# A decoder step in float32 on one core: the variance and the first products of every LayerNorm's refinement kept in PSUM

## The chip, the cores and the metric

One core of one Trainium2 chip runs the whole step as one program. The metric is the device time of one execution in microseconds, as the median of several. 0.2% of it, 2.3 us, is about what a measurement of this kernel can tell from no change.

## The reference

Two layers, each a token mixer and a gated ConvFFN, and behind each of the four a LayerNorm of the residual sum. Layer 0 mixes by sliding-window attention, layer 1 by gated linear attention (GLA). 512 prompt tokens and 8 decode tokens go through, 1024 features each.

```
def layer_norm(x, g, b):
    mu = mean(x);  var = mean((x - mu)**2)
    return (x - mu) * rsqrt(var + LN_EPS) * g + b

for i in range(2):
    m = attention(x) if i == 0 else gla(x)        # with state and cache for the decode tokens
    x = layer_norm(ALPHA * x + m, ...)
    x = layer_norm(ALPHA * x + conv_ffn(x), ...)
```

## The kernel before

Tokens lie in the free dimension, features in the 128 partitions. The 520 tokens are two groups: `a` has 256 and `b` has 264. Weights come as units of 128 output features (512 KB each); TensorE multiplies a unit with one group into an `accp` tile of PSUM, of which there are four. A float32 product is three passes of split operands (`wh`, `wl` for the weights, `xh`, `xl` for the activations), 24 matmuls of 256 or 264 columns for a unit of depth 1024. A new unit comes through a `raw` buffer, from which ScalarE (ACT) rounds `wh` (L167, L181) and VectorE (DVE) takes the rest, `wl` (L170, L183).

Group `a` runs up to five units ahead of group `b`; a method `order` writes that order out. Work that depends on a product is put into a queue of generators and emitted some units later. The framework then schedules the emitted instructions by its own model of time, so that each engine has one fixed list and waits at its head. A PSUM tile is given out in that schedule when an older one of the same name is released.

PSUM has eight banks: four `accp`, and four small ones: `sc` twice, `tp` and `pv` once each. `sc` also holds the attention scores, the first mean estimate of a norm (L256), and in GLA the product of the decay (`gla_decay`, L745: `z` times `wa2`).

`ln_end` ends a norm for one group. TensorE makes the mean `e1` and the mean square `e2` (L290), ACT squares the mean (`q`), DVE forms the negated variance `nv = (q - eps) - e2` (L306), ACT takes Ln and Exp of it to a first reciprocal root `r` (L315, L316), and three DVE operations refine it by one Newton step and leave the factor `rp` in the `pv` bank (L322, L323, L325). GpSimd (POOL) subtracts the mean from six of the eight feature blocks meanwhile (L305). Then DVE scales each block (L352), ACT writes `xh` (L353), DVE writes `xl` (L354), and the next unit's product can read them. `ln_end` is called eight times: four norms by two groups. `last` is true for the two calls of the final norm, which already take a form of their own.

After the FFN norm of layer 0, GLA starts. Its first unit is a small product of rank 16 (`gla_rank`, L736), which ACT copies to `z`; `gla_decay` makes `z` into decay factors by a chain of small operations: the product L745, `dmn` (L749, L753), `de` (L750 to L752), a scan `dcum` (L754), `eb`, `ep`, `em`. `q_a` (L779) and `k_a` (L786) need `ep` and `em` and release their `accp` tiles. Group `a` runs its units rank, q, k, v0, v1 and g0 before group `b` runs its rank product. ACT's copies L803 (`v_a`) release the tiles of v0 and v1.

Of the kernel before, what the change touches and what calls it, by code (L numbers as in the profile page):

```python
# [97 lines left out]
class Net:  # L98
# [186 lines left out]
    def ln_end(self, g, i, last=False):  # L285
# [6 lines left out]
                nc.tensor.matmul(e, self.ones_a, rest, start=False, stop=True)  # L292
        t = lambda name, b=1: self.ln.tile([P, NT - 256], F32, name=name, bufs=b)[:, :n]
        mu, q, nv, r = t("mu"), t("msq"), t("nv"), t("r")
        if last:

            nv, vr = self.mtile("sc")[:, :n], self.mtile("sc")[:, :n]
        if last:
# [15 lines left out]
                    nc.vector.tensor_tensor(x[:, m], x[:, m], e1, op=ALU.subtract)  # L314
        nc.scalar.activation(r, nv, AF.Ln, scale=-1.0)  # L315
        self.exp = nc.scalar.activation(r, r, AF.Exp, scale=-0.5).ins  # L316
        if last:
            nc.vector.tensor_tensor(vr, nv, r, op=ALU.mult)
            q = nv
            nc.vector.scalar_tensor_tensor(q, vr, 0.5, r, op0=ALU.mult, op1=ALU.mult)  # L320
        else:
            nc.vector.tensor_tensor(q, r, r, op=ALU.mult)  # L322
            nc.vector.scalar_tensor_tensor(q, q, 0.5, nv, op0=ALU.mult, op1=ALU.mult)  # L323
# [848 lines left out]
```

## Time and profile before

| | |
|---|---|
| Median of three runs | 1134.33 us (1134.12 to 1135.64) |
| The profiled execution: time, span | 1135.32 us, 1133.6 us |
| TensorE (PE) busy in the span | 1103.5 us |
| VectorE (DVE) busy | 778.8 us |
| ScalarE (ACT) busy | 565.4 us |
| GpSimd (POOL) busy | 320.2 us |
| Granted TensorE clock, mean | 0.993 |

The profiled execution lies 1.7 us above its span and 1.0 us above the median. A busy TensorE is not one at its peak, since the ends of matmuls are modelled: what counts there is the distance from start to start and the gaps with a named releaser.

### The profile page before, as it was taken

The numbers are of one execution on the slowest core, as the hardware profiler recorded it, in microseconds if no ns is written. First come the engines' busy times: TensorE is split into PE (matmuls) and PEld (weight loads), VectorE is DVE, ScalarE is ACT, GpSimd is POOL, SyncE is SP. The second block draws the span as 40 slices with busy tenths as digits, with TensorE's granted clock in tenths as the row PEclk, the third lists the DMA queues.
The fourth block names the chain that finished last, engine by engine and source line by source line (L and its number), as shares of the span: only waits on it lengthen the run. The fifth ranks groups of instructions, "written<-read, shape, count | busy, mean of one in ns | idle before, by whom it ended". The sixth has DMA issues, their size and how long they took to land.

```text
span 1133.6 us, 22916 instructions
## 1 busy us (share of the span) xinstructions
PE 1103.5 (97%) x8806; PEld 1053.7 (93%) x8806; DVE 778.8 (69%) x1626; ACT 565.4 (50%) x1251; POOL 320.2 (28%) x591
## 2 busy tenths in 40 slices
PE   8998999999999999999999999999999999999996
PEld 7997799999999999999899999899999999999995
DVE  7897679755665566568867778779755665566565
ACT  5677556524553245435455556356524553245433
POOL 3575584400110010255211101274400110001253
PEclk9999999999999999999899999999999999999999
DMA  7553023333233223242124365432333223223222
GB/s 239 152 176 99 17 76 94 112 97 127 94 98 108 93 97 110 75 134 92 58 90 146 120 177 160 138 111 94 113 95 129 94 95 110 95 95 111 76 64 76
DMA packets 53804, 122.81 MB, mean 108 GB/s; under 512 B 6808, under 2 KB 27328, under 8 KB 53696
## 3 DMA queue, kind: packets, MB, share of 16 engines
q1 hardware_dynamic: 51536, 119.47, 33.0%
q10 hardware_dynamic: 2160, 1.89, 0.5%
q8 instruction: 69, 1.13, 0.4%
q14 instruction: 39, 0.32, 0.1%
HBM read 108.67 MB, written 8.47 MB: 103 GB/s over the span
## 4 chain that ended last, share of the span: by engine, by line
PE 73%; DVE 12%; DMA 7%; ACT 3%; issue 2%; POOL 2%; SPq 1%; ACTq 0%; DVEq 0%; POOLq 0%
PE accp L221 15%; PE accp L198 15%; PE accp L200 15%; PE accp L202 15%; PE accp L222 8%; DMA vb<-dv 3%; DMA raw<-in_w_qkv 1%; DVE xs_a L354 1%; DVE wl L183 1%; DMA qs<-hl 1%; DVE sgla L909 1%; DVE wl L170 1%; DMA raw<-in_w_up 1%; DVE de L924 1%; DVE x_a L352 1%
## 5 line engine op out<-in xcount | busy, mean ns | idle before, releaser
L170 DVE TENSOR_TENSOR wl<-raw,wh 128x1024 fp32r<-128x1024 f32 (+2 forms) x172 | 207.0, 1205 | 103.9 <-ACT wh L167 103.0
L167 ACT ACTIVATE wh<-raw 128x1024 fp32r<-128x1024 f32 (+2 forms) x168 | 173.7, 1034 | 202.2 <-PE accp L200 187.6
L198 PE MATMUL accp<-xh_b,wh 128*128 128x264 f32 x976 | 272.5, 279 | 1.9 <-ACT xh_b L353 1.9
L202 PE MATMUL accp<-xh_b,wl 128*128 128x264 f32 x976 | 270.8, 277 | 0.0
L200 PE MATMUL accp<-xl_b,wh 128*128 128x264 f32 x960 | 266.5, 278 | 0.0
L221 PE MATMUL accp<-xs_a,wh 128*128 128x512 f32 x576 | 196.3, 382 | 0.0
L198 PEld LDWEIGHTS accp<-xh_b,wh 128*128 128x128 f32 x976 | 184.8, 189 | 3.4 <-ACT xh_b L353 2.5
L202 PEld LDWEIGHTS accp<-xh_b,wl 128*128 128x128 f32 x976 | 184.5, 189 | 0.9 <-issue 0.6
L200 PEld LDWEIGHTS accp<-xl_b,wh 128*128 128x128 f32 x960 | 181.6, 189 | 2.5 <-issue 0.4
L222 PE MATMUL accp<-xs_a,wl 128*128 128x256 f32 x576 | 145.4, 273 | 0.0
L198 PE MATMUL accp<-hh_b,wh 128*128 128x264 f32 x480 | 133.4, 278 | 1.7 <-ACT hh_b L228 1.2
L200 PE MATMUL accp<-hl_b,wh 128*128 128x264 f32 x480 | 133.7, 279 | 0.3 <-DVE hl_b L593 0.2
L202 PE MATMUL accp<-hh_b,wl 128*128 128x264 f32 x480 | 132.9, 277 | 0.0
L221 PEld LDWEIGHTS accp<-xs_a,wh 128*128 128x128 f32 x576 | 109.1, 189 | 11.4
L222 PEld LDWEIGHTS accp<-xs_a,wl 128*128 128x128 f32 x576 | 110.2, 191 | 1.9
L198 PE MATMUL accp<-xs_a,wh 128*128 128x256 f32 x400 | 107.5, 284 | 1.5 <-ACT wh L167 0.8
L200 PE MATMUL accp<-xs_a,wh 128*128 128x256 f32 x384 | 102.8, 281 | 0.4 <-DVE xs_a L229 0.3
L198 PEld LDWEIGHTS accp<-hh_b,wh 128*128 128x128 f32 x480 | 90.9, 189 | 2.4 <-ACT hh_b L228 1.6
L200 PEld LDWEIGHTS accp<-hl_b,wh 128*128 128x128 f32 x480 | 90.8, 189 | 1.8 <-DVE hl_b L593 0.4
L202 PEld LDWEIGHTS accp<-hh_b,wl 128*128 128x128 f32 x480 | 90.7, 189 | 0.2
L232 POOL COPY hist<-aext 128x2 f32<-128x2 f32 x44 | 10.0, 227 | 282.3 <-DVE aext L640 276.2
L198 PEld LDWEIGHTS accp<-xs_a,wh 128*128 128x128 f32 x400 | 77.1, 193 | 3.0 <-ACT wh L167 1.2
(338 smaller groups left out, 2509.2 us busy)
## 6 DMA issues: line engine op xcount, KB each, us to landing
raw<-in_w_up SPq DMA_DIRECT2D x88, 512.0 KB, 3.4
raw<-in_w_down SPq DMA_DIRECT2D x32, 512.0 KB, 3.4
raw<-in_w_gla SPq DMA_DIRECT2D x24, 512.0 KB, 3.4
raw<-in_w_mix_o SPq DMA_DIRECT2D x16, 512.0 KB, 3.9
raw<-in_w_down SPq DMA_DIRECT2D x16, 384.0 KB, 3.1
qs<-hl SPq DMA_DIRECT2D x64, 64.0 KB, 2.1
sgla<-in_state_gla SPq DMA_DIRECT2D x16, 256.0 KB, 2.7
vb<-dv SPq DMA_DIRECT2D x16, 256.0 KB, 3.9
```

Of the source, the lines that this page charges most:

```text
L167: nc.scalar.activation(h[:, c], r[:, c], AF.Copy)
L170: nc.vector.tensor_tensor(l[:, c], r[:, c], h[:, c].bitcast(F32), op=ALU.subtract)
L183: self.nc.vector.tensor_tensor(l, r, h.bitcast(F32), op=ALU.subtract)
L198: nc.tensor.matmul(o, h[:, ks], xh, start=k == 0, stop=False)
L200: nc.tensor.matmul(o, h[:, ks], xl, start=False, stop=False)
L202: nc.tensor.matmul(o, l[:, ks], xh, start=False, stop=not tail and k == nt - 1)
L221: both = lambda: nc.tensor.matmul(o, h[:, ks], in_turn(rs[:, k].rearrange("p t q j -> p t (q j)")), start=k == 0, stop=last)
L222: low = lambda: nc.tensor.matmul(o[:, :P], l[:, ks], in_turn(rh[:, k]), start=False, stop=False)
L352: v = nc.vector.scalar_tensor_tensor(x[:, m], x[:, m], sc(m), rp, op0=ALU.mult, op1=ALU.mult)
L354: xl = nc.vector.scalar_tensor_tensor(g.xl[:, m], parted(x[:, m]), bi(m), g.xh[:, m].bitcast(F32), op0=ALU.add, op1=ALU.subtract)
L909: late(nc.vector.scalar_tensor_tensor(s[:, j], vb[:, j], kraw[:, b:b + 1], s[:, j], op0=ALU.mult, op1=ALU.add))
L924: nc.vector.reciprocal(e, e)
```

## The change

The flag that chose the two PSUM tiles and the other grouping of the Newton step for the final norm alone is set for all norms. For the six other calls, `nv` moves from SBUF to an `sc` bank; the first product of the refinement becomes `nv * r` into a second `sc` bank (`vr`), in place of `r * r` in SBUF; the second becomes `vr * 0.5 * r` into the bank of `nv`, in place of `(r * r) * 0.5 * nv` in SBUF. The number of instructions is the same. Nothing else is edited.

```
         mu, q, nv, r = t("mu"), t("msq"), t("nv"), t("r")
-        if last:
+        banks = True
+        if banks:
             nv, vr = self.mtile("sc")[:, :n], self.mtile("sc")[:, :n]
...
-        if last:
+        if banks:
             nc.vector.tensor_tensor(vr, nv, r, op=ALU.mult)
             q = nv
             nc.vector.scalar_tensor_tensor(q, vr, 0.5, r, op0=ALU.mult, op1=ALU.mult)
         else:
             nc.vector.tensor_tensor(q, r, r, op=ALU.mult)
             nc.vector.scalar_tensor_tensor(q, q, 0.5, nv, op0=ALU.mult, op1=ALU.mult)
```

Each of these norms now takes both `sc` banks, from its variance to its factor. The schedule is made anew with that, and instructions move at one place above all: the FFN norm of layer 0 for group `b`, beside the start of GLA for group `a`. Line numbers behind L294 are higher by one in the changed kernel.

TensorE there, before: the decay's product L745 stands just ahead of the mean products of group `b` (the L205 and L198 rows are products of group `a`'s units).

```order
L200 MATMUL accp<-xs_a,wh 128x256
L205 MATMUL accp<-xs_a,wl 128x256 x3
L745 MATMUL sc<-z_a,wa_7008 128x256
L290 MATMUL tp<-s_b,ones_a 128x264
L205 MATMUL accp<-xs_a,wl 128x256
L290 MATMUL pv<-s_b,ones_a 128x264
```

And in the changed kernel, where the same product (L746) stands 39 rows further on, as the second instruction of unit g0:

```order
L200 MATMUL accp<-xs_a,wh 128x256
L205 MATMUL accp<-xs_a,wl 128x256 x8
L198 MATMUL accp<-xs_a,wh 128x256
L746 MATMUL sc<-z_a,wa_7016 128x256
L200 MATMUL accp<-xs_a,wh 128x256
L198 MATMUL accp<-xs_a,wh 128x256
```

It needs a bank of `sc`, and waits for the DVE operation L321, the last that reads `vr`. The other units' rows around it are unchanged up to group `b`'s rank product.

VectorE at the same place, before: the norm of `b` (L306, L322, L323, L325, L352) and the decay of `a` (L749, L753, L754) take turns.

```order
L749 TENSOR_SCALAR dmn<-sc,par 128x256
L306 SCALAR_TENSOR_TENSOR nv<-msq,pv 128x264
L314 TENSOR_TENSOR x_b<-x_b,tp 128x264 x2
L183 TENSOR_TENSOR wl<-raw,wh 128x1024
L322 TENSOR_TENSOR msq<-r 128x264
L753 TENSOR_TENSOR dmn<-dmn,de 128x256
L323 SCALAR_TENSOR_TENSOR msq<-msq,nv 128x264
L754 SCALAR_TENSOR_TENSOR dcum<-reset,dmn 128x256
L325 SCALAR_TENSOR_TENSOR pv<-msq,r 128x264
L758 COPY bl<-dcum 128x2
L841 COPY ebl<-eb 128x1
L352 SCALAR_TENSOR_TENSOR x_b<-x_b,par,pv 128x264 x8
```

After: the norm goes through in one piece, and the decay follows it.

```order
L307 SCALAR_TENSOR_TENSOR sc<-msq,pv 128x264
L315 TENSOR_TENSOR x_b<-x_b,tp 128x264 x2
L183 TENSOR_TENSOR wl<-raw,wh 128x1024
L319 TENSOR_TENSOR sc<-sc,r 128x264
L321 SCALAR_TENSOR_TENSOR sc<-sc,r 128x264
L326 SCALAR_TENSOR_TENSOR pv<-sc,r 128x264
L353 SCALAR_TENSOR_TENSOR x_b<-x_b,par,pv 128x264 x8
L355 SCALAR_TENSOR_TENSOR xl_b<-x_b,par,xh_b 128x264 x3
L750 TENSOR_SCALAR dmn<-sc,par 128x256
L355 SCALAR_TENSOR_TENSOR xl_b<-x_b,par,xh_b 128x264 x5
L754 TENSOR_TENSOR dmn<-dmn,de 128x256
L755 SCALAR_TENSOR_TENSOR dcum<-reset,dmn 128x256
```

ScalarE there, before: `eb` (L756, which needs the decay's scan) stands ahead of the first `xh_b` and of the second copy `v_a`.

```order
L752 ACTIVATE de<-de,eps 128x256
L803 COPY v_a<-accp 128x256
L756 ACTIVATE eb<-dcum 128x4
L353 ACTIVATE xh_b<-x_b,par 128x264 x2
L803 COPY v_a<-accp 128x256
L353 ACTIVATE xh_b<-x_b,par 128x264 x6
L762 ACTIVATE ep<-dcum 128x256
L763 ACTIVATE em<-dcum 128x256
L738 COPY z_b<-accp 128x264
```

After: the whole chain of `de`, `eb`, `ep` has moved behind the eight `xh_b`.

```order
L317 ACTIVATE r<-r 128x264
L804 COPY v_a<-accp 128x256
L354 ACTIVATE xh_b<-x_b,par 128x264 x3
L804 COPY v_a<-accp 128x256
L354 ACTIVATE xh_b<-x_b,par 128x264 x5
L751 ACTIVATE de<-sc,par 128x256
L752 ACTIVATE de<-de 128x256
L753 ACTIVATE de<-de,eps 128x256
L739 COPY z_b<-accp 128x264
L167 ACTIVATE wh<-raw 128x1024
L757 ACTIVATE eb<-dcum 128x4
L763 ACTIVATE ep<-dcum 128x256
```

Behind this place the instructions of all of GLA, some 1800 rows of TensorE, stand in a new order, with the same work, up to the second or third unit of layer 1's FFN; from there on TensorE has the same rows again. In the norm of layer 1's mixer, which lies in that stretch, group `a`'s scalings and splits (L353, L355) are mixed more finely with the other group's residual sums. At the attention norm of layer 0 and in group `a`'s half of the FFN norm of layer 0, the order of DVE and ACT is that of before, operation for operation.

## Rows read from the trace of the kernel before

**Rows 1.** The page's first part: busy time, share and instructions by engine.
```profile
PE 1103.5 (97%) x8806; PEld 1053.7 (93%) x8806; DVE 778.8 (69%) x1626; ACT 565.4 (50%) x1251; POOL 320.2 (28%) x591
```

**Rows 2.** What TensorE waited for, whole span: total us, times, longest.
```profile
PE accp L736 <- ACT v_a L803: 2.6, 1, 2.6
...
PE accp L198 <- ACT xh_b L353: 1.9, 2, 0.9
...
PE tp L290 <- DVE s_b L282: 1.0, 3, 0.4
...
PE accp L205 <- DVE xs_a L354: 0.5, 1, 0.5
```

**Rows 3.** Stretches: PE, PEld, DVE, ACT, POOL busy (count); clock, DMA share, GB/s.
```profile
541.00:556.00 15.00, 12.33 (x55) 10.27 (x54) 12.06 (x32) 7.79 (x18) 0.51 (x1) 0.66 0.15 54
556.00:745.00 189.00, 186.77 (x1563) 177.20 (x1563) 141.54 (x333) 98.56 (x254) 35.22 (x48) 1.00 0.43 136
1111.00:1114.00 3.00, 3.00 (x29) 3.00 (x29) 2.62 (x7) 0.99 (x3) 3.00 (x5) 1.00 0.00 0
6.00:9.00 3.00, 1.94 (x11) 1.23 (x10) 2.06 (x5) 2.13 (x6) 1.13 (x3) 1.00 1.05 339
```

**Rows 4.** TensorE in order of time, 531 to 556 us: start, duration, instruction.
```profile
531.52 0.60 PE L745 MATMUL sc<-z_a,wa 128*128 128x256 f32 x2
...
540.99 1.06 PE L205 MATMUL accp<-xs_a,wl 128*128 128x256 f32 x8
544.64 3.13 PE L736 MATMUL accp<-xh_b,wh 128*128 128x264 f32 x8 [2.59 <-ACT v_a L803]
...
550.55 1.22 PE L794 MATMUL sc<-q_a,k_a 128*128 128x128 f32 x4
...
552.92 0.56 PE L198 MATMUL accp<-xs_a,wh 128*128 128x256 f32 x1
...
555.60 0.28 PE L198 MATMUL accp<-xh_b,wh 128*128 128x264 f32 x1
```

**Rows 5.** VectorE in order of time, 537 to 547 us.
```profile
537.33 1.78 DVE L183 TENSOR_TENSOR wl<-raw,wh 128x1024 fp32r<-128x1024 f32 x1
539.04 0.97 DVE L322 TENSOR_TENSOR msq<-r 128x264 f32<-128x264 f32 x1
...
540.83 0.98 DVE L323 SCALAR_TENSOR_TENSOR msq<-msq,nv 128x264 f32<-128x264 f32 x1
...
542.33 0.41 DVE L325 SCALAR_TENSOR_TENSOR pv<-msq,r 128x264 f32<-128x264 f32 x1
...
543.66 2.48 DVE L352 SCALAR_TENSOR_TENSOR x_b<-x_b,par,pv 128x264 f32<-128x264 f32 x6
```

**Rows 6.** ScalarE in order of time, 542 to 552 us.
```profile
542.44 0.21 ACT L756 ACTIVATE eb<-dcum 128x4 f32<-128x4 f32 x1 [3.86 <-DVE dcum L754]
...
544.24 0.35 ACT L803 COPY v_a<-accp 128x256 f32<-128x256 f32 x1
544.49 2.64 ACT L353 ACTIVATE xh_b<-x_b,par 128x264 fp32r<-128x264 f32 x6
...
550.79 1.06 ACT L167 ACTIVATE wh<-raw 128x1024 fp32r<-128x1024 f32 x1
```

**Rows 7.** VectorE in order of time: group `a`'s FFN norm of layer 0.
```profile
516.41 0.60 DVE L322 TENSOR_TENSOR msq<-r 128x256 f32<-128x256 f32 x1 [0.27 <-ACT r L316]
516.94 0.41 DVE L250 TENSOR_TENSOR x_b<-x_b,accp 128x264 f32<-128x264 f32 x1
...
517.92 0.85 DVE L325 SCALAR_TENSOR_TENSOR pv<-msq,r 128x256 f32<-128x256 f32 x1
```

**Rows 8.** VectorE in order of time: group `a`'s final norm, with PSUM tiles.
```profile
1111.98 0.43 DVE L318 TENSOR_TENSOR sc<-sc,r 128x256 f32<-128x256 f32 x1 [0.31 <-ACT r L316]
1112.44 0.43 DVE L320 SCALAR_TENSOR_TENSOR sc<-sc,r 128x256 f32<-128x256 f32 x1
```

**Rows 9.** The page's fifth part, costliest groups: busy, mean ns of one; idle before, releaser.
```profile
L170 DVE TENSOR_TENSOR wl<-raw,wh 128x1024 fp32r<-128x1024 f32 (+2 forms) x172 | 207.0, 1205 | 103.9 <-ACT wh L167 103.0
```

More of the change, by code (lines that the diff above doesn't have):

```diff
@@ L294, in ln_end @@
         mu, q, nv, r = t("mu"), t("msq"), t("nv"), t("r")
-        if last:
+        banks = True
+        if banks:
             nv, vr = self.mtile("sc")[:, :n], self.mtile("sc")[:, :n]
@@ L316, in ln_end @@
         self.exp = nc.scalar.activation(r, r, AF.Exp, scale=-0.5).ins
-        if last:
+        if banks:
             nc.vector.tensor_tensor(vr, nv, r, op=ALU.mult)
```

## The prediction

> **What bounds the kernel now.** The page's first part says TensorE: 1103.5 of 1133.6 us [rows 1]. A busy TensorE is not one at its peak, so I looked next for stretches of few matmuls. Between 556 and 745 us, in GLA, 1563 matmuls start in 189 us, one every 0.121 us, at clock 1.00. [...] 55 at 0.121 us need 6.7 us, so 8.3 us are lost in that one place, where group `b`'s FFN norm of layer 0 meets GLA's start. TensorE's waits give its start: 2.59 us ahead of group `b`'s rank product L736, the longest wait in the list, put down to the copy `v_a` [rows 2, 4].
>
> ScalarE shows why that copy is late. It started at 544.24, behind two `xh_b` and behind `eb`, for which the engine had waited 3.86 us [rows 6]. `eb` needs the scan of group `a`'s decay, which took turns on VectorE with the three slow Newton operations of `b`: 0.97 us at 539.04, 0.98 at 540.83, 0.41 at 542.33 [rows 5]. The rank product, which then started at 544.64, had 16 matmuls, and took until 550.55 because it was fed by `xh_b` and `xl_b` one block at a time. The clock fell meanwhile: at 552.92 a matmul of 256 columns takes 0.56 us, at 555.60 it is 0.28 again [rows 4].
>
> **The change, part by part.**
>
> *The operations themselves.* Same count, so only durations matter. The same norm formula with PSUM tiles stands in the final norm: 0.43 us each, 0.46 from start to start [rows 8], and POOL was busy for all 3.00 us around it [rows 3]. The old ones take 0.97 and 0.98 while POOL is busy; POOL works only 0.51 us after 541 [rows 3], and the third one, behind that, takes 0.41 [rows 5]. So what is saved is the slowing beside POOL, not the operation. For group `a`, before: 516.41 to 517.92+0.85 = 518.77, or 2.36 us, with one residual sum between (0.34 to the next start) [rows 7]. After: 3 x 0.45 + 0.34 = 1.69. Each such chain is shorter by 0.67 us. Bounds: nothing, if the new ones are slowed like the old; 1.0, if the residual sum slips out of the chain.
>
> The rows say that with PSUM such an operation costs 0.43 us where one undisturbed with SBUF takes 0.41, a difference of 0.02 us [rows 5, 8]. [...]
>
> *The place at GLA's start.* The order of the work moves here: the decay's product now waits for a bank of `sc` until the norm's second Newton operation, so the norm of `b` runs through and the decay follows. I walk through it with today's times, then shift. VectorE's `wl` begins at 537 and ends at 538.6 or so (1.78 us from 537.33 today, 0.4 sooner without the decay's `dmn` ahead of it). Three operations of 0.45 end at 539.95, where today the factor was ready at 542.75 [rows 5]. The first scaling (0.41 each, 2.48 for six) starts at 540.0 instead of 542.85, the first `xh_b` at 540.4 (0.44 each, 2.64 for six [rows 6]). The second `v_a` stands behind three of them: 540.4 + 1.3 + 0.35 = 542.1. Eight matmuls of 256 columns take 1.06 us, one alone 0.28: (1.06 - 0.28) / 7 = 0.112 from start to start. Unit g0 ends at 540.99 + 8 x 0.112 = 541.9 today [rows 4]; with the decay's product in it and its wait for the bank (up to 0.4), at 542.5. So **the wait of 2.59 us is gone**.
>
> The rank product is still paced. The last `xh_b` is written at 540.4 + 8 x 0.44 + 0.35 = 544.3; the last `xl_b` after eight scalings, three splits (544.5), one `dmn` and five splits, at 547.1. It ends at 547.2, today 550.5. Then something else is late: ScalarE's `z_b` (0.38) and `wh` (1.06 [rows 6]) come before unit g1 can go on, at 548.65: a wait of 1.5 us for TensorE, which is behind group `b`'s queue of products too. g1 has 24 matmuls: 2.7 us, to 551.35. VectorE's `wl` (1.2 [rows 9]), a decay operation, `ep` and `q_a` (0.4 each) end at 551.1, in time. In this order g1 is done ahead of L794 and the next decay product. Today, by 555.60, these and three transposes were done and 16 of the 24 [rows 4]: so there is 1.2 us still owed (estimated from L745's 0.60 and about half of L794's 1.22 at the low clock), and 0.9 us done in advance (8 x 0.112). The point that answers to 555.60 is 551.35 + 1.2 - 0.9 = 551.7: **3.9 us** gained. That takes for granted that the clock stays up: TensorE waits 1.5 us and is paced for 4.7, where it did wait 2.59 and was paced for 5.9. The kernel's start, with 11 matmuls in 3 us at 6 to 9 us, has clock 1.00 [rows 3], so thin work alone does not lower it at once.
>
> *Ahead of it.* Group `a`'s FFN norm, 0.67 us shorter, lets `xs_a` and all that hangs on it start earlier: **0.7**.
>
> *The two mixer norms.* TensorE waits there for `s_b`, `xs_a` and `xh_b`: 1.0, 0.5 and 1.9 us in all the kernel [rows 2], 3.4 less 0.2 that belongs to the FFN norm. A shorter chain in `a` takes part of it. Group `b`'s chain also waits on ScalarE and a queue of products, so I take 0.6 at each norm, **1.2**, between 0 and 3.2.
>
> *Sum:* 3.9 + 0.7 + 1.2 = 5.8 us. The profiled execution took 1135.32, 1.0 above the median, so 1134.33 - 5.8 = **1128.5**. All that could go: 8.3 + 0.7 + 3.2 = 12.2, or 1122.
>
> **The rivals.**
>
> *The clock falls all the same (R1).* For it: rank `b` stays paced, and 1.5 us are waited. Today the clock was not back until 554.6, after 4 us of work from 550.55 (half speed: 2 us lost). Against it: the row at 6 to 9 us. Price 2.0: 1130.5. [...]
>
> *The decay comes too late (R2, slower).* Its product moves from 531.52 to about 539.5. Today from there to L794, which needs `k_a`, it took 19.0 us [rows 4]. Until `q_a` and `k_a`, two of four `accp` tiles are held, and the next unit of `b` waits for one. By 19 us again, that is 558.5, 6.8 behind the 551.7 above, and the clock falls for 2.0: +8.8 - 5.8 = +3.0, 1137.3. It decides from a chain of 16 us on (11.6 in my walk). Against it: today's chain lay in turns with the norm and waited for that; in the new order it is at the end of the same list.
>
> *The new order in GLA costs what is won (R3).* 1800 rows are moved, and today's 189 us behind the place have almost no waits at TensorE (0.121 us a matmul, where 0.112 is the spacing without). New waits of 5 us, a rank or decay product late in two or three pairs of units, would give 1134.
>
> *It does not do what it says (R4).* The PSUM operations are slowed like the old ones (0.97 each): the factor comes 1.6 us later than in my walk, rank `b` ends at 548.7, and no mixer norm gains; about 2.3 remain: 1132.0. Against it: rows 8, with POOL busy throughout.
>
> **How the numbers follow.** My forecast 0.50; R1 0.20; R3 0.13; R2 0.10; R4 0.07. The predicted time is the first: 1128.5. Its own range: mixer norms at 0 (1129.7) to most of their waits and g1's wait gone (1125). The range of 8 in 10 takes in R1 and R4 and stops short of R2 and most of R3: up to 1133.5, which is the forecast with the clock's 2.0, no gain at mixer norms and 1.7 us of new waits. Below, 1124.5: 9.8 of the 12.2. 0.2% is 2.3 us: faster needs under 1132.1. That holds in the forecast, in R1 and in about half of R4 with a little of R3: 0.75. Slower (over 1136.6) is R2: 0.10. The rest, 0.15, is no measurable change.
>
> **What the changed profile would show.** Right: L319 and L321 at 0.43 to 0.46 us in all norms; no wait of over 0.5 us at L737 for `v_a`; rank `b` from about 542.5 to 547 (less 0.7); a wait of about 1.5 us ahead of g1 put down to `wh`; clock 1.00 between 541 and 556, or at least 0.9; waits at `s_b`, `xs_a` and `xh_b` 1 us less in all. Wrong: a clock under 0.8 there (R1); a wait of several us for `q_a` or `k_a` or for `ep` (R2); the gain at 556 us gone again by 745 (R3); the new operations over 0.8 us (R4).

## The result

The changed kernel is slower: 1138.59 us, the median of 8 runs (1136.49 to 1142.40), against 1134.22 for the kernel before (8 runs, 1133.81 to 1135.64). The ratio is 1.0034, 95% interval 1.0023 to 1.0044, so 2.6 to 5.0 us were lost where 5.8 were to be won. The profiled execution of the changed kernel lies 2.7 us above its median, that of the kernel before 1.0 above its own.

| | before | changed |
|---|---|---|
| The profiled execution: time, span | 1135.32, 1133.6 us | 1141.28, 1139.6 us |
| TensorE waits between 541 and 556 us | 2.6 | 1.4 |
| TensorE waits between 556 and 790 us | 4.0 | 8.2 |

The first view is the stretch that the prediction was about (columns as in [rows 3]), and the same for what follows it, to the end of layer 1's mixer norm.

```profile
541.00:556.00 15.00, 13.23 (x80) 11.18 (x79) 10.36 (x27) 7.38 (x18) 0.00 (x0) 0.89 0.11 37
556.00:790.00 234.00, 225.81 (x1857) 213.96 (x1856) 179.74 (x402) 126.39 (x308) 60.77 (x85) 0.99 0.40 126
```

80 matmuls lie between 541 and 556 us, where it was 55 [rows 3] (the 8.3 us of the prediction are the 15 us of that row less 55 x 0.121): the place has become better, as forecast. The 234 us behind it hold 1857. The row of the kernel before has 1922:

```profile
556.00:790.00 234.00, 229.87 (x1922) 218.83 (x1922) 182.12 (x408) 125.54 (x307) 64.07 (x86) 1.00 0.40 126
```

65 fewer there and 25 more ahead of it leave 40, and 40 at 0.12 us are 4.8 us, lost in a part of the kernel for which the sum of the prediction had no term but the gain at the mixer norm. What TensorE waited for there, in the changed kernel (total us, times, longest):

```profile
PE accp L198 <- ACT xh_b L354: 1.6, 1, 1.6
PE accp L198 <- ACT hh_b L228: 1.6, 1, 1.6
PE pv L290 <- DVE s_a L283: 1.0, 1, 1.0
PE accp L205 <- DVE xs_a L355: 0.8, 3, 0.5
PE tp L815 <- DVE sg L935: 0.8, 1, 0.8
PE pv L840 <- DVE sp L839: 0.7, 1, 0.7
PE accp L198 <- DVE sg L927: 0.7, 1, 0.7
PE accp L198 <- DVE q_a L780: 0.5, 1, 0.5
PE sc L256 <- DVE x_b L252: 0.3, 1, 0.3
PE accp L200 <- DVE hl_b L229: 0.2, 1, 0.2
```

They sum to 8.2 us. The same list of the kernel before has 4.0, with 0.9 for `xh_b` and 0.7 for `hh_b`, and no entry for `sp`, `q_a` or `s_a`.

GLA's start itself went as it was walked through. VectorE in the norm of `b`, which answers to [rows 5]:

```profile
538.16 0.43 DVE L319 TENSOR_TENSOR sc<-sc,r 128x264 f32<-128x264 f32 x1
538.62 0.44 DVE L321 SCALAR_TENSOR_TENSOR sc<-sc,r 128x264 f32<-128x264 f32 x1
539.09 0.44 DVE L326 SCALAR_TENSOR_TENSOR pv<-sc,r 128x264 f32<-128x264 f32 x1
539.65 3.29 DVE L353 SCALAR_TENSOR_TENSOR x_b<-x_b,par,pv 128x264 f32<-128x264 f32 x8
```

ScalarE (compare [rows 6]): `eb` stands behind, and the second `v_a` comes 2.6 us sooner than at 544.24.

```profile
540.17 1.55 ACT L354 ACTIVATE xh_b<-x_b,par 128x264 fp32r<-128x264 f32 x3 [2.59 <-DVE x_b L353]
541.63 0.35 ACT L804 COPY v_a<-accp 128x256 f32<-128x256 f32 x1
541.88 2.30 ACT L354 ACTIVATE xh_b<-x_b,par 128x264 fp32r<-128x264 f32 x5
...
547.03 0.38 ACT L739 COPY z_b<-accp 128x264 f32<-128x264 f32 x1 [0.99 <-PE accp L737]
547.31 1.06 ACT L167 ACTIVATE wh<-raw 128x1024 fp32r<-128x1024 f32 x1
```

TensorE there (compare [rows 4]):

```profile
541.32 1.06 PE L205 MATMUL accp<-xs_a,wl 128*128 128x256 f32 x8
542.22 2.40 PE L737 MATMUL accp<-xh_b,wh 128*128 128x264 f32 x8
544.45 2.54 PE L737 MATMUL accp<-xl_b,wh 128*128 128x264 f32 x8
548.42 0.38 PE L198 MATMUL accp<-xs_a,wh 128*128 128x256 f32 x1 [1.42 <-ACT wh L167]
548.63 0.28 PE L200 MATMUL accp<-xs_a,wh 128*128 128x256 f32 x1
...
549.04 0.42 PE L198 MATMUL accp<-xs_a,wh 128*128 128x256 f32 x1
...
552.83 0.28 PE L198 MATMUL accp<-xh_b,wh 128*128 128x264 f32 x1
```

No wait for `v_a`; rank `b` from 542.22 to about 547; 1.42 us of waiting for `wh`. But from 549 on the matmuls of g1 take 0.42 us in place of 0.28: the granted clock, 1.00 from 542.22 to 547 us, is 0.50 from 549.1 to 552.3, and the 24 of them take 548.42 to 552.83, 4.4 us in place of 2.7. By 555.1 TensorE had done all that the kernel before had done by 555.60, ten matmuls of q0_b and g1's last eight besides: 18 x 0.112 = 2.0 us of work. That makes 2.5 us, and 2.9 counted from the FFN norm's start, where this execution lay 0.42 behind: of 4.6 forecast here (3.9 + 0.7), 1.7 went to the clock.

### The profile page after: what moved, and what is told of

It reads as the page before. It is cut to its first block, busy times and chain, and to the rows that moved or that the text cites. A ratio compares the mean times of both kernels' runs of the same rounds, so it can differ in the third digit from the quotient of the medians.

```text
span 1139.6 us, 22907 instructions
## 1 busy us (share of the span) xinstructions
PE 1107.3 (97%) x8806; PEld 1056.8 (93%) x8806; DVE 777.9 (68%) x1626; ACT 565.8 (50%) x1251; POOL 313.7 (28%) x591
## 4 chain that ended last, share of the span: by engine, by line
PE 73%; DVE 12%; DMA 6%; ACT 4%; issue 2%; POOL 1%; SPq 1%; DVEq 0%; ACTq 0%; POOLq 0%
PE accp L221 15%; PE accp L198 15%; PE accp L200 15%; PE accp L202 15%; PE accp L222 8%; DMA vb<-dv 3%; DVE wl L170 1%; DVE de L925 1%; DVE xs_a L355 1%; DMA raw<-in_w_up 1%; DMA qs<-hl 1%; DVE sgla L910 1%; DVE wl L183 1%; DVE x_a L353 1%; DMA raw<-in_w_qkv 1%
## 5 line engine op out<-in xcount | busy, mean ns | idle before, releaser
L198 PE MATMUL accp<-xh_b,wh 128*128 128x264 f32 x976 | 272.9, 280 | 3.5 <-ACT xh_b L354 2.9
L198 PEld LDWEIGHTS accp<-xh_b,wh 128*128 128x128 f32 x976 | 185.4, 190 | 5.1 <-ACT xh_b L354 3.6
L198 PE MATMUL accp<-hh_b,wh 128*128 128x264 f32 x480 | 134.2, 280 | 2.6 <-ACT hh_b L228 2.1
L198 PE MATMUL accp<-xs_a,wh 128*128 128x256 f32 x400 | 108.3, 286 | 2.7 <-ACT wh L167 2.2
L200 PE MATMUL accp<-xs_a,wh 128*128 128x256 f32 x384 | 104.4, 285 | 0.4 <-DVE xs_a L229 0.3
L198 PEld LDWEIGHTS accp<-hh_b,wh 128*128 128x128 f32 x480 | 92.0, 192 | 3.2 <-ACT hh_b L228 2.5
L198 PEld LDWEIGHTS accp<-xs_a,wh 128*128 128x128 f32 x400 | 78.0, 195 | 4.3 <-ACT wh L167 2.8
```

The lines of the kernel that those rows point to most:

```text
L198: nc.tensor.matmul(o, h[:, ks], xh, start=k == 0, stop=False)
L200: nc.tensor.matmul(o, h[:, ks], xl, start=False, stop=False)
```

## The experiments

The study's first theory, **O**: the loss comes of the new order of instructions behind GLA's start, by the waits that this order has, and lapses of the clock that follow some of them. **N**: the PSUM form itself delays the mixer norms. **C**: lapses that come by chance. Later ones are named where they arise.

The kernels were measured in four series, in which the kernel before had medians of 1134.2 to 1136.7 us; the ratios to it in the same series are what to compare. The absolute times of the expectations take no account of these differences. "Lag" is worked out from the traces: how much later the same instruction starts than in the profiled execution of the kernel before, less that difference at the first L290 of layer 0's FFN norm (513.69 us there). "Rank" is group `b`'s rank product (544.64), "third z" the decay product of `a` at 593.87, "end" the first L256 of the last norm (1070.11). The waits are TensorE's from 556 to 790 us, the clock is that of 541 to 556.

| kernel | median | ratio (95%) | lag: rank | third z | end | waits | clock |
|---|---|---|---|---|---|---|---|
| changed | 1138.59 | 1.0034 (1.0023 to 1.0044) | -2.84 | -0.38 | 5.13 | 8.2 | 0.89 |
| e1 only `b` FFN | 1141.81 | 1.0053 (1.0039 to 1.0067) | -2.51 | 1.02 | 5.19 | 9.3 | 0.77 |
| e2 all but `b` FFN | 1134.57 | 0.9988 (0.9979 to 0.9997) | -0.57 | 0.04 | -1.01 | 3.5 | 0.66 |
| e3 in `pv` | 1132.17 | 0.9970 (0.9958 to 0.9981) | -1.25 | -1.01 | -1.95 | 3.6 | 0.66 |
| e4 changed, two `vb` | 1135.95 | 1.0009 (0.9999 to 1.0019) | -2.83 | -0.36 | 1.79 | 7.0 | 0.89 |
| e5 in `pv`, two `vb` | 1131.75 | 0.9974 (0.9962 to 0.9985) | -1.32 | -2.32 | -4.44 | 2.9 | 0.77 |
| e6 one `sc` bank | 1138.93 | 1.0039 (1.0024 to 1.0054) | -2.77 | -0.31 | 2.94 | 8.0 | 0.89 |
| e7 `pv`, rank thrice | 1132.09 | 0.9970 (0.9958 to 0.9982) | -1.29 | -3.27 | -3.64 | 3.7 | 1.00 |
| e8 changed, rank thrice | 1134.38 | 0.9981 (0.9970 to 0.9992) | -2.79 | -3.22 | -3.38 | 4.0 | 1.00 |
| e9 `pv`, both | 1131.03 | 0.9950 (0.9931 to 0.9968) | -1.29 | -3.27 | -4.18 | 3.9 | 1.00 |

**e1 and e2: the change in one call, and in the other five.**

```
-        banks = True
+        banks = last or (i == 1 and g.i)            # e1
+        banks = last or not (i == 1 and g.i)        # e2
```

> The form with two sc banks in one call alone: group b's FFN norm of layer 0; the other five norms as before. Its order of instructions is that of the changed kernel from GLA's start on, but for few rows. Theory O (the new order behind GLA's start costs the time, by waits of TensorE and the lapses of the clock that follow them): nearly the whole loss, 1138 to 1140 us, with TensorE waits of over 1 us ahead of hh_b near 738 us and xh_b near 786 us. Theory N (the PSUM form itself delays the two mixer norms): these norms are as before, so the GLA start's gain of about 2 to 3 us is all there is: 1131 to 1133 us. Theory C (lapses of the clock that come by chance, wherever): 1134 to 1140 with a wide spread and no common place of the lapses.

> The complement: five norm calls with two sc banks, group b's FFN norm of layer 0 as before. TensorE's order is that of the kernel before in every row. Theory O: a small gain, 0.57 us from group a's FFN norm and about 0.2 from each mixer norm: 1133.0 to 1134.0 us, clock mean 0.993 as before. Theory N: slower than before by 2 us or more, with the waits of 1.6 us for xh_b and 1.0 for s_a at layer 1's mixer norm as in the changed kernel. Theory C: a spread of several us.

The one call that moves the order carries the whole loss (1.0053, at 1141.81 even above the expected range); the five others together gain a little (0.9988; the 1134.57 us lie above the expected 1133.0 to 1134.0, in a series where the kernel before had 1135.37). N is out: with the same PSUM norm at layer 1's mixer, e2 waits 0.88 us for `xh_b`, as before, and e1, with the old SBUF norm there, 1.91:

```profile
781.37 0.38 PE L198 MATMUL accp<-xh_b,wh 128*128 128x264 f32 x1 [0.88 <-ACT xh_b L354]
```
```profile
787.12 0.38 PE L198 MATMUL accp<-xh_b,wh 128*128 128x264 f32 x1 [1.91 <-ACT xh_b L354]
```

C is weakened too: in e1's trace no lapse lies between 556 and 790 us (clock 1.00), and yet it loses 4.2 us from the third z to the end. The changed kernel, whose profiled execution had two lapses there (clock 0.50 from 740.5 to 743 and from 788.5 to 791 us), loses 5.5. Waits alone suffice for most of it.

```profile
556.00:790.00 234.00, 224.75 (x1865) 212.53 (x1864) 179.79 (x402) 126.07 (x308) 61.81 (x85) 1.00 0.39 126
```

**e3: the same operations, no further bank.** Variance, both products and factor lie one over the other in the bank of `e2`.

```
-            nv, vr = self.mtile("sc")[:, :n], self.mtile("sc")[:, :n]
+            nv, vr = (self.mtile("sc")[:, :n], self.mtile("sc")[:, :n]) if last else (e2, e2)
```

> All six norm calls with PSUM operands, but no further bank: nv, both products and the factor all lie in e2's pv bank, one over the other. The order of instructions is that of the kernel before on TensorE, GpSimd and SyncE, and but for one place of v_a on ScalarE. Theory O: the operations take 0.43 to 0.46 us, the norm of b at GLA's start gets its factor about 1.0 us earlier (the two slow ones lie between, the decay's operations stay in turns), so the wait of 2.6 us for v_a shrinks to about 1.6 to 2; with 0.6 from group a's FFN norm and the mixer norms 1131.5 to 1133.5 us. Theory N: no gain, or slower. If the PSUM operations are slowed by reading and writing one bank in place, they take over 0.6 us and the time is that of before.

Faster than the kernel before by 0.3%, in the middle of the forecast; so the operations do what the change was made for, if no bank is taken from the decay. Their durations (min/median/max), here and in the changed kernel:

```profile
L319 DVE TENSOR_TENSOR pv<-pv,r x6: 427/430/433, 159.4 to 776.2; 128x256 f32<-128x256 f32 x3, 128x264 f32<-128x264 f32 x3
```
```profile
L319 DVE TENSOR_TENSOR sc<-sc,r x8: 427/432/442, 159.4 to 1130.1; 128x256 f32<-128x256 f32 x4, 128x264 f32<-128x264 f32 x4
```

In place or in two banks they take 0.43 us, and the third operation (L326) takes as much with POOL idle (0.43 in the changed kernel at 184.9 and 784.2 us). The wait for `v_a` shrank to 1.90 us, within the expected 1.6 to 2.

**e4 and e5: one wait of the new order taken out.** Theory **V**, for the largest wait that is not in a norm. VectorE in the changed kernel, ahead of `hh_b`:

```profile
729.39 0.95 DVE L910 SCALAR_TENSOR_TENSOR sgla<-vb,kraw,sgla 128x256 f32<-128x256 f32 x1
730.27 0.41 DVE L252 SCALAR_TENSOR_TENSOR x_a<-x_a,accp 128x256 f32<-128x256 f32 x1
730.60 0.62 DVE L910 SCALAR_TENSOR_TENSOR sgla<-vb,kraw,sgla 128x256 f32<-128x256 f32 x1
...
735.46 0.88 DVE L910 SCALAR_TENSOR_TENSOR sgla<-vb,kraw,sgla 128x256 f32<-128x256 f32 x2 [1.86 <-DMA vb<-dv]
736.26 0.42 DVE L283 TENSOR_TENSOR s_a<-s_a,sq 128x256 f32<-128x256 f32 x1
736.60 0.48 DVE L935 SCALAR_TENSOR_TENSOR sg<-tp,par,sg 128x256 f32<-128x256 f32 x1
```

`vb` has one buffer. Its next transfer starts when the second `sgla` has read it, and in the new order one and the other of these stand apart, at 729.39 and 730.60. The transfer lands at 735.4, VectorE stands still for 1.86 us until then, and `sg`, for which TensorE waits by way of `hh_b`, is queued behind. In the kernel before VectorE stood for `vb` too, 1.69 us, but the pair stood together (1.41 us in place of 1.83) and began 2.7 us earlier, and `sg` came at 733.71:

```profile
726.70 1.41 DVE L909 SCALAR_TENSOR_TENSOR sgla<-vb,kraw,sgla 128x256 f32<-128x256 f32 x2 [0.34 <-ACT sgla L908]
...
732.25 0.48 DVE L909 SCALAR_TENSOR_TENSOR sgla<-vb,kraw,sgla 128x256 f32<-128x256 f32 x1 [1.69 <-DMA vb<-dv]
...
733.71 0.48 DVE L934 SCALAR_TENSOR_TENSOR sg<-tp,par,sg 128x256 f32<-128x256 f32 x1
```

Both experiments give `vb` a second buffer in the last head, e4 in the changed kernel, e5 in e3's.

```
-            vb = self.gp.tile([P, 2, 256], F32, name="vb")
+            vb = self.gp.tile([P, 2, 256], F32, name="vb" if h < GH - 1 or p % 2 else "vb2")
```

> The changed kernel with a second buffer for vb in the last GLA head, so that its transfers from dv start before the previous vb is used up. Up to group a's mixer norm of layer 1 TensorE, VectorE and ScalarE have the changed kernel's order. Theory V (the wait of 1.58 us for hh_b near 738 us comes of VectorE standing at sgla for vb, with sg behind it): the wait for hh_b falls under 0.7 us, the clock has no lapse behind it, and the time is 1 to 2.5 us below the changed kernel's: 1136 to 1137.5 us. Rival: something else on VectorE's or ScalarE's list is nearly as late (sg's own transposes, sq), the wait stays over 1.2 us and the time at 1138.5.

> The form in the pv bank (the previous experiment's kernel of 1132.2 us) with the same second vb buffer; the order of all engines but SyncE is unchanged. Theory V: its wait of 0.76 us for hh_b goes or halves: 1131.2 to 1131.8 us, if no later wait takes it up. Rival: the mixer norm behind waits longer by as much, 1132.2.

e4: the wait for `hh_b` is 0.22 us instead of 1.58, no lapse follows (clock 1.00 from 556 to 745 and from 745 to 790 us), and 1.0034 becomes 1.0009, 2.8 us, a little more than the 1 to 2.5 expected. V holds for this wait. It isn't worth all of the 2.8: by the L256 near 738 us, up to which TensorE's order is the same, the lag has become 1.5 us better (0.53 to -1.01). The other 1.8 of the 3.3 at the end lie behind, where e4's trace has no lapse up to 790 us, and where 55 rows of TensorE in the mixer norm stand elsewhere than in the changed kernel. That norm still waits, 1.5 for `xs_a` and 1.5 for `xh_b`. e5: the wait is no longer listed in its trace, but 0.9974 can't be told from e3's 0.9970, though the 1131.75 us lie in V's range. Where the order was good there is little to win.

**e6: one bank in place of two.**

```
-            nv, vr = self.mtile("sc")[:, :n], self.mtile("sc")[:, :n]
+            nv, vr = (self.mtile("sc")[:, :n], self.mtile("sc")[:, :n]) if last else [self.mtile("sc")[:, :n]] * 2
```

> All six norms with PSUM operands in one sc bank: variance, both products one over the other. The decay's product of group a moves too, but by only some 27 rows of TensorE (about 3 us) in place of 40, and the scheduler makes a third order behind it. Theory O1 (a new order behind the place costs by the waits that it happens to have): a time clearly different from both, 1133 to 1139 us. Theory O2 (it is the lateness of the decay, 7.6 us, that costs): nearer to the form in the pv bank, 1131.5 to 1133.5 us, with fewer new waits behind 556 us in proportion.

1.0039, as slow as the change, with the decay's product less late (28 matmuls later than before, in the changed kernel 58, which are the 39 rows of the listing, where like ones share a row; its start is 3.7 and 7.2 us later, counted as lags). So neither the second bank nor the full lateness is needed. The expectation was wrong on one point: this is no third order. In the two traces TensorE, VectorE, ScalarE and GpSimd have the same rows in the same order from 563 us on, and 39 rows of TensorE between 535 and 559 us are all that differ on it. That is why the time is not "clearly different from both": the same order far behind, with about half the lateness, has the same loss. The range of O1 holds 1138.93; O2's doesn't.

**e7, e8 and e9: the clock, and the order of before.** Group `b`'s rank product is done three times over and scaled by a third.

```
-            for k in range(KD):
+            for j, k in enumerate([k for k in range(KD) for _ in range(3 if g.i else 1)]):
...
-        nc.scalar.copy(g.z, ps)
+        nc.scalar.activation(g.z, ps, AF.Copy, scale=1 / 3) if g.i else nc.scalar.copy(g.z, ps)
```

> The form in the pv bank, where group b's rank product does each of its 16 matmuls three times and z is scaled by a third: TensorE is kept busy while it is fed block by block, and rank b still ends with the last xl_b. Some 230 rows behind stand in another order. Theory K (the clock falls because of the thin rank product): the granted clock between 541 and 556 us is 0.9 or more, g1's matmuls follow at 0.11 us, and the stretch to the first matmul of q0_b is shorter by about 2.0 us. Rival: the clock falls all the same after the wait of 1.9 us that stands ahead of the product, and nothing is gained there (or rank b ends later).

> The changed kernel (two sc banks in all six calls), with group b's rank product done three times over and z scaled by a third. The longer rank product makes the scheduler come back to the order of the kernel before: the decay of group a is as late as in the changed kernel (its product is the second instruction of g0, its chain stands behind the eight xh_b), but behind GLA's first pair of heads, some 180 rows of TensorE on, all engines have the order of the kernel before to the end. Theory O1 (the new order far behind costs, by the waits that it has at layer 1's output projection and mixer norm): waits there as before (0.7 for hh_b, 0.9 for xh_b), 1130 to 1133 us. Theory O2 (the late decay itself costs, or two banks do): 1136 us or more, with the loss at GLA's start.

> The form in the pv bank with both helpers: rank b done three times over (z scaled by a third), and the second vb buffer in the last head. If the two gains seen in the traces add (2.3 us from the clock at GLA's start, about 1 from hh_b): 1129 to 1130.5 us. Rival: they don't show in the median, since waits elsewhere (xh_b at the mixer norms, k_b) or chance lapses of the clock in other places take them up: 1131.5 to 1132.2 us, as either one alone.

e7 in the stretch (the clock is the third column from the end):

```profile
541.00:556.00 15.00, 13.34 (x111) 12.68 (x110) 13.43 (x35) 9.20 (x22) 0.57 (x2) 1.00 0.13 45
```

Theory K holds: with a fed TensorE the clock stayed up (1.00, where e3 has 0.66) in spite of 1.54 us of waiting ahead of the product, and e7 gains 2.26 us on e3 by the third z (lags -3.27 and -1.01). In the medians this doesn't show (0.9970 for both): its size lies within what the two intervals leave open.

e8 is the decisive one. It has the change's two banks and its late decay; TensorE even waits 1.87 us for `k_a`:

```profile
541.78 2.87 PE L737 MATMUL accp<-xh_b,wh 128*128 128x264 f32 x24
544.48 2.86 PE L737 MATMUL accp<-xl_b,wh 128*128 128x264 f32 x24
549.21 0.71 PE L795 MATMUL sc<-q_a,k_a 128*128 128x128 f32 x4 [1.87 <-DVE k_a L787]
```

But behind the first pair of heads it has the order of before (TensorE's rows are the same from 575 us on), and there its waits are 4.0 us, as before, and its time is 0.9981.

```profile
556.00:790.00 234.00, 229.92 (x1927) 219.06 (x1926) 180.89 (x409) 126.53 (x306) 62.81 (x88) 1.00 0.41 128
```

From the third z to the end its lag changes by -0.2 us; in the changed kernel by 5.5. The median, 1134.38, lies above the expected 1130 to 1133 in a series where the kernel before had 1136.71. The thrice-done product itself accounts for 2 to 3 us at GLA's start, by the clock. That is not all of the 6.0 us (0.0053) by which e8 is faster than the changed kernel (3.5 at the near ends of the two intervals), and it lies ahead of the third z. O1 stands, O2 falls.

e9 joins e7 and e5: 0.9950, 5.7 us below the kernel before of the same series, the fastest of all and a version that beats both kernels. Its 1131.03 us lie between the two expected ranges, and its interval overlaps those of e3, e5 and e7 a little, so that the two gains add is not shown.

## Why the prediction was wrong

- **The operations: right.** 0.43 to 0.44 us in every norm (425 to 442 ns), forecast 0.43 to 0.46; the old third one, undisturbed, took 0.41 to 0.43. From the SBUF to the PSUM form that is 0.03 us more at most. Group `a`'s chain at the FFN norm is 0.61 us shorter (1.75 in place of 2.36, forecast 0.67), and 0.57 of it reached the next L290.
- **The 2.59 us wait: right, and the walk behind it to within 0.5 us.** Factor ready at 539.5 (539.95 forecast), `v_a` at 542.0 (542.1), rank `b` ended at about 547.0 (547.2), g1 at 548.42 (548.65), `q_a` done at 550.9 (551.1).
- **"That takes for granted that the clock stays up": wrong, R1 came true.** The clock was 0.89 in the stretch, between the 0.9 of the forecast's sign and the 0.8 of R1's, and 1.7 us went (R1's price was 2.0). The row at 6 to 9 us [rows 3] was a poor witness. In all eight kernels with the thin rank product the clock fell here (0.66 to 0.89 from 541 to 556 us); in the three with the filled one it did not (1.00). The two levels that the traces show are 1.00 and 0.50: in the kernel before it was 0.50 from 545 to 554.6 us, in the changed one from 549.1 to 552.3. What in the thin product brings it down is not shown.
- **The mixer norms: 0.6 each was about right, where the order was kept.** From the lags between 720 and 1070 us, 0.8 at layer 1 in e3 and 0.5 in e2. At layer 0 group `a`'s chain gave 0.56 up to group `b`'s L290 in the changed kernel, of which 0.37 went again ahead of `xh_b` (1.32 us of waiting, 0.95 before). At layer 1 the changed kernel lost in place of gaining.
- **The step that failed: the sum put the new order behind GLA's start at nothing.** The prediction named it as R3, "the new order in GLA costs what is won", gave it 0.13 and left it out of the sum. No reason for leaving it out is given; all that it says of this stretch is that "today's 189 us behind the place have almost no waits". That tells how good the old order is, and nothing of a new one; read rightly, it says that a new order has hardly anything to win there and 4 us or more to lose. The waits rose from 4.0 to 8.2 us. Of the 2.9 us won by 555 us, 0.4 were left at the third z: 1.2 of the 2.5 that went are the waits for `sp` and `q_a`, the rest no single wait shows. From there the lag went from -0.38 to 5.13. R3's sign, the gain gone by 745, was seen (a lag of 0.53 at the L256 near 738 us). Its price, "new waits of 5 us", was close to the 4.2 that the waits grew by, but set against a gain of 5.8 it would still have left 1133.5 by that sum (the prediction says 1134), and so no loss. The gain never came to that, since the clock took 1.7 of it, and at layer 1's mixer norm, where 0.6 was to be won, the new order waits longer.
- **R2, the late decay: not the cause.** Its chain took 11.8 us from the product to `q_a` (539.1 to 550.9; 11.6 forecast), and e8 has it as late without the loss. That R2's 1137.3 us come nearest to the measured time is chance. **R4:** out, the operations are fast.

What stays open: e4 shows what one wait costs. From the third z to the end e4 still loses 2.2 us, where e8 loses none. By the lists they lie in GLA and in layer 1's mixer norm, but those waits weren't taken out one by one. (The rest of the 0.0028 between e4 and e8 is, by the traces, the filled rank product's: their lags at the third z are -0.36 and -3.22.) Of the 5.5 us that the changed kernel's trace loses there, a part belongs to its two lapses from 740 and 788 us: e1 and e6 have none and lose 4.2 and 3.3. So lapses are not proper to the order, and how many of the eight timed executions had them isn't known; their mean granted clock goes from 0.990 in the slowest (1142.40 us) to 0.995 in the fastest (1136.49), which fits lapses as a part of the spread.

## What to carry to other kernels

Where a scheduler makes the order, taking a shared buffer for longer is a change of the whole order behind it: compare the two orders first, and where they differ far on, the walk through one place is no forecast of the time. A stretch almost without waits is a risk then, not a cover. Put intermediate values over one that is dead already (e3) before taking a second buffer.

## What was not expected of the hardware

- An operation of VectorE with one input in SBUF and the other in PSUM kept 0.43 to 0.44 us beside a busy GpSimd in the changed kernel's norms (GpSimd was busy for all of the 1.44 us from 538.16 to 539.60 us, in which three of them ran), where in the kernel before those with two SBUF inputs took 0.60 to 0.98 while GpSimd was busy (throughout, but for the 0.98 at 540.83 us, where it was for 0.68), and 0.41 and 0.43 where it was idle (542.33 and 184.49 us). Not every operation with two SBUF inputs was slow beside a busy GpSimd: the sum `s_a` took 0.42 us in the kernel before, at 494.57 us, while GpSimd ran memsets for all of it.
- The clock also fell without a cause that the traces show. In eight of the eleven profiles, that of the changed kernel among them, it was lower for some microseconds from about 135 us on (0.50 from 135.9 to 139.1 us in the changed kernel), in the attention layer, where all have the same order and the wait ahead of it is 0.5 us (0.54 in both kernels). The granted clock from 134 to 142 us is 0.79 in the changed kernel's profile and 1.00 in that of the kernel before. It costs 1.6 us (the changed kernel, 1.08 us ahead of the kernel before at 127 us, is 0.56 behind at 142). After equal waits of 1.5 to 1.9 us near 738 and 786 us it fell in the changed kernel (0.72 from 738 to 744 us, 0.68 from 786 to 791) and not in e1 (1.00 in both) or e6 (1.00 from 556 to 790). Within one kernel the times spread by 2 to 6 us.
- TensorE's busy time grew with the loss, 1103.5 to 1107.3 us, with the same matmuls, some of them at the lower clock: it can't be read as work.
